# Opening of a decoder-layer kernel: three products side by side, two weights ahead of the second chunk, sums of squares ranked higher, later attention units six steps on

## The chip, the cores and the metric

The kernel runs on one core of one Trainium2 chip. The metric is device time in microseconds (us). Before the change the median of three runs is 1660.32 us (1659.6 to 1661.01). A core has a tensor engine (PE in the profile; PEld is its weight load), a vector engine (DVE), a scalar engine (ACT), GpSimd (POOL) and a sync engine (SP) that here only issues DMAs. Each engine works through its own queue strictly in order; a semaphore holds an instruction until what it reads, or the buffer that it overwrites, is ready.

## What is computed

One step of a hybrid decoder layer, for a prompt of 1024 tokens and, with the same weights, for 8 samples of 8 tokens (1088 columns in all). Cut to what the change touches:

```python
xn = rmsnorm(x, norm1_g)
proj = xn @ w_in
q, k, v, glu_a, glu_b, gate_a, gate_b = jnp.split(proj, SPLIT_IDX, axis=-1)
# branch A: attention over a window of 128, with a sink per head
s = einsum(q, k) * HEAD_DIM ** -0.5;  p = softmax(concat[where(mask, s, NEG_INF), sinks])
branch_a = (p[..., :-1] @ v) @ w_o_attn
# branch B: gated linear unit, causal depthwise convolution of 31 taps
u = glu_a * sigmoid(glu_b)
branch_b = silu(layernorm(dwconv(u))) @ w_pb
h = x + (sigmoid(gate_a) * branch_a + sigmoid(gate_b) * branch_b) @ w_out
...
```

The model is 1024 wide, with 16 heads of 64 (4 key heads); the feed-forward part that follows is 2816 wide.

## The kernel before

**Products.** All arithmetic is fp32. Each fp32 product is made of three matmuls (`mm3`, L200 to L202 in the profile): operands are split in a high part rounded to the tensor engine's fp32r form and the rest, and high x high, low x high and high x low are summed. A weight piece of 128 output channels by 1024 inputs comes by DMA (`wraw`), ACT casts it to `whi` (L181) and DVE subtracts to get `wlo` (L182). A product over one chunk of columns is 8 slices of the inputs x 3 = 24 matmuls into one PSUM bank. There are two rings of four banks: "mm" and "aux".

**Opening (`phase_x`).** The 1088 columns come in chunks of 384, 384 and 320 (c = 0, 1, 2). For each chunk `norm1_raw` makes the split of x times the norm's gain (`xh` on ACT, L263; `xl` on DVE, L264), and `norm1_stats` the squares (ACT, L272) and their running sum over the eight slices (DVE, L274); `rstd_rows` then turns the sum into a row of 1/rms: mean matmuls on PE (L292), a root on ACT and a `RECIPROCAL` on DVE (L310, L311, tile `rows`), matmuls that spread `rows` over all partitions (L296), a copy on ACT (L298, `rstd`). Five first products (glu_b, glu_a, a query piece, gate, a second query piece) are taken of the not yet normalized x, so that PE needn't wait for the norm; their evacuations multiply by `rstd` (L819 `u`, L822 `c`, L827 `qt`, L711 `gt`). Their weights are `whi`/`wlo` twice, then `whix`, `whiy`, and one that is kept in the tile `q`. For c = 0 the first two products run side by side, slice by slice, as the data lands. Later `norm1` scales x itself (DVE, L304), casts (ACT, L305) and subtracts on DVE or POOL (L307), in place, for the products that follow.

**Order.** The program is written as a stream, and a scheduler makes each engine's queue from it by priorities; `with self.later(n)` pushes the instructions inside n places back. The sums and `rstd_rows` stand under `MEAN_LATER[c]` (L277), the convolution's multiply-adds (L480, the "macs", which fill DVE through the whole middle) under `CONV_LATER` = 1200. After this the order is fixed: an engine that waits for one instruction doesn't start the next.

**Attention.** `plan_units` (from L788) lays the attention units of a pass p between the matmuls of the products, in steps of three matmuls. A unit has for each of its two head groups g: `scores` (L356, L357, into two aux banks), the softmax (DVE L327 and L334, ACT L332 and L336), `turn` (four transposes per block of keys on PE, L366, into one aux bank, then ACT writes `pth` and DVE `ptl` from it, L229 and L230), and `mix` (L378, L379). An aux bank is free again when DVE has made `ptl` from it. Unit 0 alone has its turns and mixes put off by `FIRST_WAIT` = (6, 14) steps; the next unit starts `SPACING` = 22 steps (19 in the second pass) behind it.

## Time and profile before

| | value |
|---|---|
| median of three runs | 1660.32 us (1659.6 to 1661.01) |
| the profiled execution's own time | 1659.53 us |
| its span, first to last instruction | 1657.8 us |
| mean granted PE clock | 0.997 |
| PE busy | 1642.9 us, 99% |
| DVE busy | 1336.1 us, 81% |
| ACT busy | 893.3 us, 54% |
| POOL busy | 328.1 us, 20% |

The span is what the trace covers; 1.73 us of the execution lie around it. PE is busy for all but 15 us of it, so the table itself says little: what matters is where these 15 us are, and where the clock was below 1. Those places are found in the list of PE's waits, the timeline of PE and the table of windows, and are shown in the prediction.

### The profile page before, as it was taken

How to read it: one execution, taken by the hardware profiler on the slowest of the kernel's cores; microseconds unless marked ns; L12 is line 12 of the kernel's file. 1: busy time of each engine (PE TensorE's matmuls, PEld its weight loads, DVE VectorE, ACT ScalarE, POOL GpSimd, SP SyncE). 2: the span in 40 equal slices, each digit the busy share in tenths (PEclk: the TensorE clock that was granted, in tenths of full speed). 3: DMA queues.
4: the chain of work that ended last, by engine and by line, in shares of the span. 5: the costliest groups of instructions: out<-in, count | busy, mean ns of one | idle time of the engine just before them, and what ended most of it. 6: DMA issues, size and time to landing. Idle time of an engine off the chain costs nothing.

```text
span 1657.8 us, 30344 instructions
## 1 busy us (share of the span) xinstructions
PE 1642.9 (99%) x11616; PEld 1627.3 (98%) x11616; DVE 1336.1 (81%) x2430; ACT 893.3 (54%) x1817; POOL 328.1 (20%) x589
## 2 busy tenths in 40 slices
PE   9999999999999999999999999999999999999998
PEld 9999999999999999999999999999999999999997
DVE  8899999999769995866685897877777777977556
ACT  7434477753488754993343564444444446834322
POOL 1210114171211211110000123333433220000050
PEclk9999999999999999999999999999999999999999
DMA  6122216254421255545346527676777544857473
GB/s 213 43 52 71 60 63 167 62 178 103 115 67 47 83 195 184 165 137 190 113 136 194 134 79 204 183 182 176 182 176 176 144 112 149 286 157 218 138 148 117
DMA packets 121313, 232.12 MB, mean 140 GB/s; under 512 B 25408, under 2 KB 67536, under 8 KB 120736
## 3 DMA queue, kind: packets, MB, share of 16 engines
q1 hardware_dynamic: 88208, 140.14, 27.6%
q0 software_dynamic: 32384, 89.51, 21.3%
q8 instruction: 91, 1.49, 0.4%
q10 hardware_dynamic: 576, 0.53, 0.1%
q14 instruction: 54, 0.44, 0.1%
HBM read 169.74 MB, written 89.62 MB: 156 GB/s over the span
## 4 chain that ended last, share of the span: by engine, by line
PE 81%; DVE 11%; ACT 4%; issue 2%; DMA 1%; POOL 0%; SPq 0%; DVEq 0%; ACTq 0%; POOLq 0%
PE mm L200 19%; PE mm L202 19%; PE mm L201 19%; PE aux L200 6%; PE aux L202 6%; PE aux L201 6%; DVE c L480 3%; DVE bt L480 2%; PE aux L366 1%; ACT p L332 1%; ACT p L336 1%; PE aux L378 1%; DVE wlo L182 1%; PE aux L356 1%; PE aux L379 1%
## 5 line engine op out<-in xcount | busy, mean ns | idle before, releaser
L200 PE MATMUL mm<-xh,whi 128*128 128x384 f32 (+1 forms) x920 | 306.6, 333 | 0.6 <-ACT whi L181 0.6
L201 PE MATMUL mm<-xl,whi 128*128 128x384 f32 (+1 forms) x920 | 301.1, 327 | 0.0
L202 PE MATMUL mm<-xh,wlo 128*128 128x384 f32 (+1 forms) x920 | 300.7, 327 | 0.0
L200 PEld LDWEIGHTS mm<-xh,whi 128*128 128x128 f32 x920 | 173.3, 188 | 2.2 <-ACT whi L181 1.2
L201 PEld LDWEIGHTS mm<-xl,whi 128*128 128x128 f32 x920 | 173.4, 188 | 1.0
L202 PEld LDWEIGHTS mm<-xh,wlo 128*128 128x128 f32 x920 | 173.1, 188 | 0.1
L1209 DVE SCALAR_TENSOR_TENSOR acc<-st,fc,acc 128x1104 f32<-128x1104 f32 x88 | 119.5, 1361 | 8.7 <-ACT acc L1207 7.9
L181 ACT CAST whi<-wraw 128x1024 fp32r<-128x1024 f32 (+1 forms) x65 | 62.7, 970 | 56.8 <-PE mm L201 44.6
L480 DVE SCALAR_TENSOR_TENSOR bt<-u,consts,bt 128x513 f32<-128x513 f32 x120 | 89.7, 747 | 0.6
L480 DVE SCALAR_TENSOR_TENSOR c<-sm,hsum,c 128x512 f32<-128x512 f32 x120 | 89.4, 745 | 0.5
L182 DVE TENSOR_TENSOR wlo<-wraw,whi 128x1024 fp32r<-128x1024 f32 (+1 forms) x65 | 72.5, 1121 | 20.1 <-ACT whi L181 19.6
L480 DVE SCALAR_TENSOR_TENSOR c<-u,consts,c 128x512 f32<-128x512 f32 x112 | 83.5, 745 | 0.2
L229 ACT CAST wlo<-th 128x512 fp32r<-128x512 f32 x56 | 35.1, 626 | 65.0 <-PE aux L202 41.3
L1378 ACT COPY st<-mm 128x272 f32<-128x272 f32 (+2 forms) x133 | 44.4, 350 | 46.8 <-PE mm L202 46.8
L200 PE MATMUL mm<-th,whi 128*128 128x272 f32 x240 | 69.3, 289 | 0.0
L202 PE MATMUL mm<-th,whi 128*128 128x272 f32 x240 | 69.3, 289 | 0.0
L201 PE MATMUL mm<-tl,whi 128*128 128x272 f32 x240 | 69.1, 288 | 0.0
L332 ACT ACTIVATE p<-p,nm 128x257 f32<-128x257 f32 (+1 forms) x128 | 62.2, 490 | 11.0 <-DVE nm L327 10.1
L1357 DVE TENSOR_TENSOR st<-st,aux 128x272 f32<-128x272 f32 (+2 forms) x95 | 34.2, 378 | 38.5 <-PE aux L202 38.5
L202 PE MATMUL mm<-sh,wlo 128*128 128x384 f32 (+1 forms) x192 | 62.6, 326 | 0.0
L201 PE MATMUL mm<-sl,whi 128*128 128x384 f32 (+1 forms) x192 | 62.6, 326 | 0.0
L200 PE MATMUL mm<-sh,whi 128*128 128x384 f32 (+1 forms) x192 | 62.6, 326 | 0.0
(651 smaller groups left out, 5906.8 us busy)
## 6 DMA issues: line engine op xcount, KB each, us to landing
wraw<-wall SPq DMA_DIRECT2D x87, 512.0 KB, 4.0
d_x<-st POOLq DMA_DIRECT2D x27, 544.0 KB, 4.9
d_wd<-wall POOLq DMA_DIRECT2D x54, 256.0 KB, 6.1
th<-wall SPq DMA_DIRECT2D x18, 512.0 KB, 6.0
wraw<-wall SPq DMA_DIRECT2D x33, 256.0 KB, 4.1
x<-d_x SPq DMA_DIRECT2D x14, 544.0 KB, 4.8
d_x<-acc POOLq DMA_DIRECT2D x9, 816.0 KB, 7.2
d_wo<-wall POOLq DMA_DIRECT2D x24, 256.0 KB, 4.9
```

The source lines that it names most:

```text
L181: self.nc.scalar.copy(h[:, z], r[:, z])
L182: self.nc.vector.tensor_tensor(l[:, z], r[:, z], h[:, z].bitcast(F32), ALU.subtract)
L200: mm(ps, wh, xh, start=first, stop=False, skip_group_check=more)
L201: mm(ps, wh, xl, start=False, stop=False, skip_group_check=more)
L202: mm(ps, wl, xh, start=False, stop=last, skip_group_check=more)
L229: self.nc.scalar.copy(h, src)
L332: nc.scalar.activation(pt[:, j, lo:width + 1], pt[:, j, lo:width + 1], AF.Exp, bias=nm[:, j:j + 1], scale=-1.0, accum_out=den[:, j:j + 1])
L336: nc.scalar.activation(pt[:, j, lo:width], pt[:, j, lo:width], AF.Identity, scale=den[:, j:j + 1])
L480: mac = lambda o, x, w: nc.vector.scalar_tensor_tensor(o, x, w, o, ALU.mult, ALU.add)
L1209: self.last_tap = nc.vector.scalar_tensor_tensor(acc, st[:, k:k + AW], fw(f, k), acc, ALU.mult, ALU.add)
L1357: plus = lambda d, s: nc.vector.tensor_tensor(d, d, s, ALU.add)
L1378: op(d, r(ps))
```

## The change

Four things are altered.

1. In chunk 0 three products run side by side instead of two (`SIDE = 3`). The third weight, which came as one load of 512 KB after all of chunk 0's x, now comes in four pieces beside the first two weights, and is split in four parts instead of two.
2. The loads: after chunk 0, SP issued all four loads of chunk 1, then weights 3 and 4, then chunk 2. Now it issues the first load of chunk 1, the two weights, then the rest of chunk 1 and chunk 2. `norm1_load` becomes a generator for this.
3. `MEAN_LATER` falls from (100, 100, 100) to (90, 95, 60), so the squares' sums and the rows of 1/rms rank higher; `norm1(0)` is called before the products of chunk 2 instead of after those of chunk 1, and `norm1(1)` after the loop.
4. In both attention passes every unit behind unit 0 starts six steps later.

```diff
-MEAN_LATER = (100, 100, 100)
+MEAN_LATER = (90, 95, 60)
 W_PARTS = 4
+SIDE = 3
...
     def norm1_load(self, pp, c):
         o, n = CHUNKS[c]
         xr = self.t(pp, [P, KT, n], f"xr{c}")
         if c == 0:
             self.w_raw += [self.t(self.wp, [P, DM], "wraw", bufs=2) for _ in range(2)]
+            self.w_raw.append(self.t(self.cv, [P, UW], "u", bufs=2)[:, :DM])
+        yield xr
         for k in range(0, KT, 2):
+            if k:
+                yield
...
     def norm1_raw(self, c, xr, xh, xl):
-        parts = list(zip(self.w_parts(W_PARTS), self.w_parts(W_PARTS))) if c == 0 else []
+        parts = list(zip(*[self.w_parts(W_PARTS) for _ in range(SIDE)])) if c == 0 else []
...
                 steps += [(at + d, f) for d, f in new]
-                at += SPACING[p][kind]
+                at += SPACING[p][kind] + (FIRST_WAIT[0] if (kind, n) == ("u", 0) else 0)
...
-        xr = [self.norm1_load(p0, 0)]
+        loads = [self.norm1_load(p0, c) for c in range(3)]
+        xr = [next(x) for x in loads]
+        for _ in loads[0]:
+            pass
         first = COFF["ident"][0]
-        self.raw_slot = lambda i: (self.cv, "u") if i == 2 else (self.wp, "wraw")
-        self.w_load()
+        self.raw_slot = lambda i: (self.wp, "wraw")
         nc.sync.dma_start(self.consts[:, first:], a["consts"][:, first:])
-        xr.append(self.norm1_load(p0, 1))
+        next(loads[1])
         while len(self.w_raw) < FIRST:
             self.w_load()
-        xr.append(self.norm1_load(p0, 2))
+        for x in loads[1:]:
+            for _ in x:
+                pass
...
             rs.append(self.norm1_stats(p0, c, xr[c]))
+            if c == 2:
+                self.norm1(0, xr[0], rs[0], xh, xl)
             self.scale = rs[c]
             evs, tags = (ev_b, ev_a, ev_q(0), gate_evac(*self.order[3]), ev_q(1)), FIRST_TAGS[c]
-            side = 0 if c else 2
+            side = 0 if c else SIDE
...
             if c == 0:
                 self.derive()
-            if c:
-                self.norm1(c - 1, xr[c - 1], rs[c - 1], xh, xl)
+        self.norm1(1, xr[1], rs[1], xh, xl)
         self.norm1(2, xr[2], rs[2], xh, xl)
```

Three places show what this does to the queues. In the names the numbers are the program's buffers; line numbers of the changed kernel are 1 to 10 higher.

The first is ACT's queue as chunk 0 ends and the fourth weight (`whiy`) is needed. `xh_20` is the high part of chunk 0, `xh_22` of chunk 1, `sq` are squares. Before:

```order
L272 ACTIVATE sq_240<-xr_29_126 128x384
L263 ACTIVATE xh_22_106<-xr_33_148,consts_77 128x384
L272 ACTIVATE sq_243<-xr_29_126 128x384
L263 ACTIVATE xh_22_106<-xr_33_148,consts_77 128x384 x7
L310 ACTIVATE rows_248<-aux_247,consts_77 128x3
L181 CAST whiy_211<-wraw_153 128x512 x2
```

Now:

```order
L268 ACTIVATE xh_22_106<-xr_33_130,consts_77 128x384
L277 ACTIVATE sq_244<-xr_29_126 128x384
L277 ACTIVATE sq_247<-xr_29_126 128x384
L182 CAST whiy_218<-wraw_154 128x512 x2
L277 ACTIVATE sq_250<-xr_29_126 128x384
L182 CAST q_26_122<-wraw_156 128x512 x2
L268 ACTIVATE xh_22_106<-xr_33_130,consts_77 128x384 x6
L315 ACTIVATE rows_255<-aux_254,consts_77 128x3
```

The two casts of `whiy` stood behind seven casts of `xh_22` and the root for chunk 0's rows; now they stand ahead of six of those and of the root, and so does the next weight.

The second is DVE's queue ahead of the `RECIPROCAL` of chunk 1's rows. `xr_29` is chunk 0's x, which `norm1` scales in place, `xl_25` the low part of chunk 2, `sq` with 320 columns chunk 2's sum. Before:

```order
L304 SCALAR_TENSOR_TENSOR xr_29_126<-xr_29_126,consts_77,rstd_57_246 128x384 x2
L264 SCALAR_TENSOR_TENSOR xl_25_109<-xr_36_157,consts_77,xh_24_108 128x320
L307 TENSOR_TENSOR xl_21_105<-xr_29_126,xh_20_104 128x384
L264 SCALAR_TENSOR_TENSOR xl_25_109<-xr_36_157,consts_77,xh_24_108 128x320 x4
L274 TENSOR_TENSOR sq_640<-sq_640,sq_638 128x320
...
L274 TENSOR_TENSOR sq_658<-sq_658,sq_655 128x320
L311 RECIPROCAL rows_446<-rows_446 128x3
L819 TENSOR_TENSOR u_162<-aux_456,rstd_76_444 128x384
```

Now:

```order
L309 SCALAR_TENSOR_TENSOR xr_29_126<-xr_29_126,consts_77,rstd_57_253 128x384
L279 TENSOR_TENSOR sq_638<-sq_638,sq_635 128x320
L312 TENSOR_TENSOR xl_21_105<-xr_29_126,xh_20_104 128x384
L279 TENSOR_TENSOR sq_641<-sq_641,sq_638 128x320
L309 SCALAR_TENSOR_TENSOR xr_29_126<-xr_29_126,consts_77,rstd_57_253 128x384 x3
L312 TENSOR_TENSOR xl_21_105<-xr_29_126,xh_20_104 128x384
L309 SCALAR_TENSOR_TENSOR xr_29_126<-xr_29_126,consts_77,rstd_57_253 128x384
L316 RECIPROCAL rows_453<-rows_453 128x3
L312 TENSOR_TENSOR xl_21_105<-xr_29_126,xh_20_104 128x384
L828 TENSOR_TENSOR u_165<-aux_463,rstd_76_451 128x384
```

The reciprocal still stands behind all seven sums of chunk 2 and all eight scalings of chunk 0; what moved is that scalings and sums now alternate, and that one of four low parts of `norm1(0)` left for DVE follows it.

The third is DVE's queue in the first attention unit. `bt` and `c` are the convolution's macs, `ptl_2134` (now `ptl_2141`) is the first turn's low part, whose aux bank a later score matmul on PE takes over. Before:

```order
L334 RECIPROCAL den_2058<-den_2058 128x4
L480 SCALAR_TENSOR_TENSOR bt_1675<-u_1495,consts_77,bt_1675 128x513
L480 SCALAR_TENSOR_TENSOR c_1673<-u_1495,consts_77,c_1673 128x512
...
L480 SCALAR_TENSOR_TENSOR c_1673<-sm_1674,hsum_86,c_1673 128x512
L480 SCALAR_TENSOR_TENSOR c_1673<-u_1495,consts_77,c_1673 128x512
L230 TENSOR_TENSOR ptl_2134<-aux_2128,pth_2133 128x512
L327 ISA p_2140,nm_2152<-aux_2141,masks_945,nsink_84 128x256
```

Now:

```order
L339 RECIPROCAL den_2065<-den_2065 128x4
L485 SCALAR_TENSOR_TENSOR bt_1682<-u_1502,consts_77,bt_1682 128x513
...
L485 SCALAR_TENSOR_TENSOR c_1680<-u_1502,consts_77,c_1680 128x512
L231 TENSOR_TENSOR ptl_2141<-aux_2135,pth_2140 128x512
L485 SCALAR_TENSOR_TENSOR c_1680<-sm_1681,hsum_86,c_1680 128x512
L485 SCALAR_TENSOR_TENSOR bt_1682<-u_1502,consts_77,bt_1682 128x513
L485 SCALAR_TENSOR_TENSOR c_1680<-u_1502,consts_77,c_1680 128x512
L183 TENSOR_TENSOR wlo_210_2163<-wraw_2006,whi_209_2162 128x1024
L231 TENSOR_TENSOR ptl_2176<-aux_2170,pth_2175 128x512
L332 ISA p_2185,nm_2197<-aux_2186,masks_952,nsink_84 128x256
```

Between the reciprocal and the first `ptl` there are eight macs in both. What moved is the score evaluation of the next unit (the `ISA` rows), which now comes after both turns: three macs, a weight's `wlo` and the second `ptl` stand before it.

## The prediction

> **What bounds the kernel now.** I read the page first, then the list of PE's waits, the table of windows around each wait, and the timelines of PE, DVE and ACT there. The page:

> ```profile
> span 1657.8 us, 30344 instructions
> PE 1642.9 (99%) x11616; PEld 1627.3 (98%) x11616; DVE 1336.1 (81%) x2430; ACT 893.3 (54%) x1817; POOL 328.1 (20%) x589
> PE 81%; DVE 11%; ACT 4%; issue 2%; DMA 1%; POOL 0%; SPq 0%; DVEq 0%; ACTq 0%; POOLq 0%
> ```

> The reader is to see that PE stands still for 14.9 us in all, so no regrouping of the same matmuls can win more than that and what the clock lost. The waits (engine, line, what was waited for; total, times, longest):

> ```profile
> PE aux L356 <- DVE ptl L230: 2.3, 2, 2.2
> PE aux L296 <- DVE rows L311: 1.5, 1, 1.5
> PE mm L200 <- ACT whiy L181: 1.2, 1, 1.2
> ```

> The change works on exactly these: 1.2 and 1.5 in the opening, 2.2 at the attention units. A wait can cost more than itself, which the windows show (length; PE, PEld, DVE, ACT, POOL busy; granted clock; DMA share; GB/s):

> ```profile
> 22.00:24.00 2.00, 2.00 (x11) 1.91 (x12) 2.00 (x6) 2.00 (x5) 0.00 (x0) 0.89 1.09 346
> 24.00:26.00 2.00, 2.00 (x8) 2.00 (x7) 2.00 (x4) 2.00 (x5) 0.00 (x0) 0.50 1.08 271
> 26.00:28.00 2.00, 2.00 (x10) 2.00 (x10) 2.00 (x6) 1.51 (x4) 0.00 (x0) 0.76 0.64 180
> 52.00:54.00 2.00, 1.72 (x12) 1.72 (x13) 0.46 (x3) 0.48 (x1) 0.00 (x0) 1.00 0.00 0
> 204.00:206.00 2.00, 1.92 (x10) 1.73 (x9) 2.00 (x8) 2.00 (x9) 0.00 (x0) 0.61 0.00 0
> 206.00:208.00 2.00, 2.00 (x8) 2.00 (x7) 2.00 (x6) 2.00 (x5) 0.54 (x1) 0.53 0.14 59
> ```

> Lost clock is length times (1 minus clock): 0.22 + 1.00 + 0.48 = 1.7 us behind the wait for `whiy`, and 0.78 + 0.94 = 1.7 behind the wait for `ptl`, each half speed for about 3.4 us. The wait for `rows` drew no such stretch: the clock stayed 1.00. So **what can be had** is 1.2 + 1.7, 1.5, 2.2 + 1.7, and at the start some of the two short waits shown below: about 8.5 us, 0.5%.

> [...]

> **The start.** Three products take 9 matmuls per slice of x where two took 6.

> ```profile
> 6.80 0.44 PE L200 MATMUL mm<-xh,whi 128*128 128x384 f32 x1 [0.25 <-ACT whi L181]
> 7.78 0.44 PE L200 MATMUL mm<-xh,whi 128*128 128x384 f32 x1 [0.38 <-ACT whi L181]
> 16.92 0.33 PE L200 MATMUL mm<-xh,whix 128*128 128x384 f32 x1
> 17.10 0.33 PE L201 MATMUL mm<-xl,whix 128*128 128x384 f32 x1
> 16.00:20.00 4.00, 4.00 (x25) 4.00 (x24) 4.00 (x12) 4.00 (x10) 0.16 (x2) 1.00 1.05 400
> ```

> Starts lie 0.173 us apart, so a slice lasts 1.56 us instead of 1.04, and PE asks for x and weights later. The same bytes come (DMA already full, share 1.05), with 512 KB of them moved ahead. I set the start at 0.2 us gained, bounds minus 0.6 (both waits gone) to plus 1 (a late piece of the third weight, about one slice of PE work).

> **The wait for `whiy`.** ACT and PE:

> ```profile
> 17.66 3.64 ACT L263 ACTIVATE xh<-xr,consts 128x384 fp32r<-128x384 f32 x7
> 21.35 1.13 ACT L181 CAST whiy<-wraw 128x512 fp32r<-128x512 f32 x2
> 22.00 0.44 PE L200 MATMUL mm<-xh,whiy 128*128 128x384 f32 x1 [1.24 <-ACT whiy L181]
> ```

> The cast moves ahead of six of the seven `xh` (6 x 0.52 = 3.1 us) and the root, so it ends near 19, with PE arriving at 20.8 as before. Its load now stands ahead of three of chunk 1's four, so it doesn't come late. I cost this wait at nothing: minus 1.24 and minus 1.7. If the load came 2 us late, the 1.2 would be back.

> **Chunk 1's rows.** This is the term that decides the opening. Without the gap, PE reaches these matmuls at about 50.8 (before: 52.28 less 1.46) minus 0.2 minus 2.9, minus five matmuls that now stand behind them (0.9): **46.8**. DVE must by then have run the reciprocal:

> ```profile
> 29.69 0.56 DVE L819 TENSOR_TENSOR u<-mm,rstd 128x384 f32<-128x384 f32 x1 [1.17 <-ACT rstd L298]
> 35.51 1.14 DVE L728 TENSOR_TENSOR q<-qt,q 64x384 fp32r<-64x384 f32 x2
> 37.62 2.96 DVE L304 SCALAR_TENSOR_TENSOR xr<-xr,consts,rstd 128x384 f32<-128x384 f32 x4
> 42.32 0.55 DVE L307 TENSOR_TENSOR xl<-xr,xh 128x384 fp32r<-128x384 f32 x1
> 45.55 2.68 DVE L264 SCALAR_TENSOR_TENSOR xl<-xr,consts,xh 128x320 fp32r<-128x320 f32 x4
> 48.15 3.98 DVE L274 TENSOR_TENSOR sq<-sq,sq 128x320 f32<-128x320 f32 x7
> 52.06 0.17 DVE L311 RECIPROCAL rows<-rows 128x3 f32<-128x3 f32 x1
> 52.28 0.93 PE L296 MATMUL aux<-consts,rows 128*128 128x128 f32 x6 [1.46 <-DVE rows L311]
> 20.00:50.00 30.00, 28.76 (x164) 28.59 (x163) 28.25 (x52) 19.67 (x43) 5.59 (x5) 0.94 0.33 100
> ```

> DVE is busy for 28.25 of these 30 us: it, not the rank of the sums, is what is late. From chunk 0's `u` to the reciprocal 22.4 us pass (29.69 to 52.06). In the new order three more sums of chunk 1 and three more `xl` of chunk 2 stand between these two and one `xl` of `norm1` fewer: by the rows above 3 x 0.57 + 3 x 0.67 - 0.5 = +3.2 us, up to 25.6. The scalings take 0.74 here, with POOL at work beside them; should all eight run at the 0.55 of the `xl` of like size, it is 8 x 0.19 = 1.5 less, 24.1. Chunk 0's `u` itself comes about 4 us sooner: before, it waited for `rstd` until 29.69, and the gap and the lost clock (2.9) and 1.2 of its own wait lay ahead of it; I take 25.6. So the reciprocal falls at 49.7 to 51.2, or at 48 if `u` comes earlier still: I take **49.7**, the end nearest to undisturbed rows. PE waits 2.9 us there instead of 1.5 (bounds 1 and 4.4), and, being longer than the 1.24 that cost clock before, it probably costs the 1.7 as well. PE then passes at 49.9, against 52.28 - 0.9 = 51.4 for the same work: **1.5 us won**, or nothing with the clock.

> **Chunk 2's rows.** The same chain again:

> ```profile
> 72.36 0.17 DVE L311 RECIPROCAL rows<-rows 80x4 f32<-80x4 f32 x1
> 72.97 1.01 PE L296 MATMUL aux<-consts,rows 80*128 80x80 f32 x8
> ```

> They now stand 58 matmuls sooner in PE's queue, at 0.173 x 320/384 = 0.144 each (estimated by columns) 8.4 us: with 0 to 1.5 won, PE comes at 72.97 - 8.4 - 1.5 = 63.1 to 64.6. On DVE, five evacuations, four parts of `q`, eight scalings and three `xl` stand between the two reciprocals, 5 x 0.56 + 4 x 0.57 + 8 x 0.74 + 3 x 0.55 = 12.7 us, so it falls at about 49.7 + 12.7 = 62.4, up to 64.5 if an evacuation waits. The wait is 0 to 1.4. With the start I carry **1 us won** out of the opening, bounds minus 0.5 and 4. The waits removed there come back as waits for DVE.

> **The attention units.** DVE and PE:

> ```profile
> 197.40 0.76 DVE L480 SCALAR_TENSOR_TENSOR bt<-u,consts,bt 128x513 f32<-128x513 f32 x1
> ...
> 202.12 0.75 DVE L480 SCALAR_TENSOR_TENSOR c<-u,consts,c 128x512 f32<-128x512 f32 x1
> 202.79 0.68 DVE L230 TENSOR_TENSOR ptl<-aux,pth 128x512 fp32r<-128x512 f32 x1
> 207.46 1.22 DVE L182 TENSOR_TENSOR wlo<-wraw,whi 128x1024 fp32r<-128x1024 f32 x1
> 203.52 0.38 PE L356 MATMUL aux<-kd,q 128*128 128x256 f32 x1 [2.15 <-DVE ptl L230]
> 50.00:80.00 30.00, 28.54 (x192) 28.23 (x192) 23.01 (x42) 15.97 (x33) 7.97 (x8) 1.00 0.18 58
> 80.00:190.00 110.00, 110.00 (x735) 109.88 (x734) 108.76 (x165) 40.30 (x82) 14.59 (x25) 1.00 0.23 59
> ```

> DVE is full from 80 to 190 (108.76 of 110 us), so whatever stands ahead of `ptl` delays it one for one. Counting the new queue with the durations of these rows, 8.5 us more of work (12 to 13 macs at 0.67) stand ahead of the first `ptl`, since macs are placed sooner; DVE's 7 idle us in 50 to 80 and the 2 before can take nearly all of it. So the first `ptl` starts near 202.5 again. The score that takes its bank moves six steps back, 18 x 0.173 = 3.1 us, and would no longer wait for it. But the later score banks now need the **second** `ptl` too, which stands behind three more macs and a `wlo` (3 x 0.67 + 1.2): 202.5 + 0.6 + 3.2 = 206.3, done at 206.9. PE comes there at about 203.5 (201.4 where it waited before, plus 3.1, less what the opening won, and some transposes and scores change places). It waits **2 to 4 us**, over the length that drew the half clock, against 2.2 before. For the same work: before, PE passed at about 208.8 with its wait and lost clock; now 206.9 and 1.7 of clock, 208.6. So what the opening won is mostly swallowed here, where DVE is the clock: cumulative gain 0 to 1.5, or 3.2 if the clock holds. The second pass moves by six steps likewise, but PE has no wait of 0.3 us there to win.

> **The sum.** 1659.53 (the profiled execution: span 1657.8 and 1.73 around it; 0.8 under the median of 1660.32, within the runs' 1.4) minus 1.0 = **1658.5 us**, no change: below 0.2% (3.3 us), about what a measurement of this kernel can tell.

> **Rivals.**
> *DVE keeps up.* If DVE recovers its idle time sooner (`rows` of chunk 1 by 47, the second `ptl` by 203.5), all three waits and both stretches of lost clock go: 1659.53 - 2.9 - 1.5 - 3.9 - 0.2 = 1651. For it: 1.75 idle us of DVE in 20 to 50 and 7 in 50 to 80; POOL's use stretches DVE's scalings (0.74 against 0.55), which may fall elsewhere. Against it: the counts above. Half of it, say only the attention wait gone, gives 1655.
> *Slower: the second `ptl`.* If a wait of over 3.4 us stands before the second unit's score, with 1.7 us of clock, and one of 4.4 with 1.7 at chunk 1's rows, then PE loses 6.1 + 5.1 where it lost 8.3 (2.9 + 1.5 + 3.9) in all: +2.9, and the later units, which are six steps nearer the end of the pass, give one more such wait (2.2 + 1.7): 1659.5 + 2.9 + 3.9 = 1666. It decides if the second `ptl` starts later than 207.5. Against it: nothing waits after that in the trace except 0.3 us here and there.
> *The loads.* If `whiy` or the third weight comes late, the opening's gap stays: 1659 to 1661, inside the forecast.

> **Chances.** Forecast (within 0.2%): 0.45. DVE keeps up, wholly or by half: 0.37, faster by over 0.2%. Slower by over 0.2%: 0.18. The forecast's own range is 1656.3 to 1662.8; for 8 in 10 it must reach to 1651.5 and to 1664.

> **What would show it.** Right: no wait of PE for `whiy`, clock 1.00 from 22 to 28; a wait at chunk 1's rows of 1 to 4 us, still for DVE's reciprocal, near 46 to 49; a wait for the second `ptl` near 203 to 207 with a clock below 1 behind it. Wrong: a wait for `rows` under 0.5 us, or PE full from 195 to 215 at clock 1.00: then the time is near 1651 to 1655. If `whiy` is waited for again, my reading of the loads was wrong.

## The result: slower by 0.44%, and the profile after

The changed kernel takes 1667.67 us (median of 6 runs, 1666.13 to 1669.55), the kernel before beside it 1660.8 us (6 runs, 1659.6 to 1662.93). The ratio is 1.0044, 95% interval 1.0033 to 1.0055. The interval leaves out 1: it is slower, and its time lies 3.7 us above the upper end of the predicted range. The profiled execution has a span of 1665.5 us, 7.7 more than before.

The page of the changed kernel, the lines that answer to those of before:

```profile
span 1665.5 us, 30349 instructions
PE 1646.9 (99%) x11616; PEld 1628.4 (98%) x11616; DVE 1336.3 (80%) x2432; ACT 892.8 (54%) x1819; POOL 325.0 (20%) x589
```

PE has the same 11616 matmuls, and is busy 4.0 us longer with them and idle 3.7 us longer. The list of PE's waits says where it was idle (engine, line, what it waited for: total, times, longest; some rows left out):

```profile
PE aux L301 <- DVE rows L316: 3.3, 2, 1.9
PE aux L361 <- DVE ptl L231: 2.9, 1, 2.9
PE aux L297 <- DVE sq L279: 1.3, 1, 1.3
...
PE aux L383 <- ACT pth L230: 0.6, 1, 0.6
...
PE mm L201 <- ACT whiy L182: 0.3, 1, 0.3
```

The wait for ACT's `whiy` went from 1.2 to 0.3 us, as the new order of ACT's queue says. In its place PE waits 1.3 us for chunk 0's last sum of squares on DVE, 1.4 and 1.9 us for chunk 1's and chunk 2's `rows`, and 2.9 us for the second `ptl`. All four are waits for DVE. The windows of the changed kernel around them (length; PE, PEld, DVE, ACT, POOL busy; clock; DMA share; GB/s):

```profile
26.00:28.00 2.00, 2.00 (x10) 2.00 (x9) 1.12 (x3) 0.98 (x3) 0.00 (x0) 0.50 1.04 352
52.00:54.00 2.00, 2.00 (x15) 2.00 (x15) 0.56 (x2) 0.49 (x2) 1.01 (x1) 1.00 0.00 0
64.00:66.00 2.00, 0.54 (x4) 0.28 (x2) 2.00 (x3) 1.23 (x4) 1.11 (x2) 1.00 0.00 0
66.00:68.00 2.00, 1.55 (x9) 1.56 (x10) 1.97 (x4) 0.51 (x1) 1.07 (x1) 0.73 0.03 8
68.00:70.00 2.00, 2.00 (x9) 2.00 (x9) 1.46 (x5) 1.90 (x3) 0.84 (x1) 0.50 0.67 205
210.00:212.00 2.00, 0.39 (x4) 0.19 (x2) 2.00 (x4) 0.00 (x0) 0.00 (x0) 1.00 0.20 82
214.00:216.00 2.00, 2.00 (x7) 1.81 (x7) 2.00 (x8) 2.00 (x9) 0.00 (x0) 0.50 0.67 238
```

In the windows where PE stands nearly still (64 to 66, 210 to 212) DVE is busy for the whole 2.00 us. Half clock follows the waits at 22, 64 and 210 us; it doesn't follow the one at 50. Before, there were two such stretches, so the third accounts for 1.7 of the 4.0 us that PE is busy longer. Most of the rest lies in the transposes of `p`, whose group is busy for 36.3 us before and for 38.7 us now:

```profile
L366 PE MATMUL aux<-consts,p 128*128 128x128 f32 x240 | 36.3, 272 | 0.2 <-DVE ptl L230 0.2
L371 PE MATMUL aux<-consts,p 128*128 128x128 f32 x240 | 38.7, 275 | 0.7 <-ACT p L341 0.2
```

At 263 us, for one, four of them take 1.53 us, where four took 0.60 before: they follow ACT, which makes the four parts of `p` that they read one by one in 1.69 us, and which had itself waited 1.91 us for POOL. This part of the loss is not DVE's, and why POOL was late there was not tried.

```profile
262.03 0.52 ACT L337 ACTIVATE p<-p,nm 128x257 f32<-128x257 f32 x1 [1.91 <-POOL p L326]
262.54 1.69 ACT L341 ACTIVATE p<-p,den 128x256 f32<-128x256 f32 x4
263.09 1.53 PE L371 MATMUL aux<-consts,p 128*128 128x128 f32 x4 [0.24 <-ACT p L341]
```

DVE's timeline shows the turn that PE waits for (start, duration):

```profile
208.81 0.69 DVE L231 TENSOR_TENSOR ptl<-aux,pth 128x512 fp32r<-128x512 f32 x1
209.41 0.75 DVE L485 SCALAR_TENSOR_TENSOR c<-sm,hsum,c 128x512 f32<-128x512 f32 x1
...
211.39 1.22 DVE L183 TENSOR_TENSOR wlo<-wraw,whi 128x1024 fp32r<-128x1024 f32 x1
212.53 0.69 DVE L231 TENSOR_TENSOR ptl<-aux,pth 128x512 fp32r<-128x512 f32 x1
```

The first `ptl` starts at 208.81, where before it started at 202.79: 6.0 us later, although the change to the attention units moves nothing ahead of it. PE is late by then too. The first unit, which the six steps don't move, has its first score at 184.57 us before and at 188.96 now, so of the 7.7 us in all 4.4 were lost ahead of the attention:

```profile
184.57 0.28 PE L356 MATMUL aux<-kd,q 128*128 128x256 f32 x1
188.96 0.28 PE L361 MATMUL aux<-kd,q 128*128 128x256 f32 x1
```

### The profile page after: what moved, and what is told of

It is laid out like the page before. It is cut to its first block, busy times and chain, and to the rows that moved or that the text cites. A ratio compares the mean times of both kernels' runs of the same rounds, so it can differ in the third digit from the quotient of the medians.

```text
span 1665.5 us, 30349 instructions
## 1 busy us (share of the span) xinstructions
PE 1646.9 (99%) x11616; PEld 1628.4 (98%) x11616; DVE 1336.3 (80%) x2432; ACT 892.8 (54%) x1819; POOL 325.0 (20%) x589
## 4 chain that ended last, share of the span: by engine, by line
PE 83%; DVE 10%; DMA 2%; ACT 2%; issue 2%; POOL 0%; SPq 0%; DVEq 0%; ACTq 0%; POOLq 0%
PE mm L201 20%; PE mm L203 20%; PE mm L202 19%; PE aux L203 6%; PE aux L201 6%; PE aux L202 6%; DVE c L485 3%; DVE bt L485 1%; PE aux L371 1%; PE aux L383 1%; DVE q L733 1%; PE aux L384 1%; PE aux L361 1%; DVE wlo L183 1%; PE aux L362 1%
## 5 line engine op out<-in xcount | busy, mean ns | idle before, releaser
L201 PE MATMUL mm<-xh,whi 128*128 128x384 f32 (+1 forms) x920 | 306.6, 333 | 0.6 <-ACT whi L182 0.5
L201 PEld LDWEIGHTS mm<-xh,whi 128*128 128x128 f32 x920 | 173.5, 189 | 2.0 <-ACT whi L182 0.8
L182 ACT CAST whi<-wraw 128x1024 fp32r<-128x1024 f32 (+1 forms) x65 | 62.6, 969 | 53.9 <-PE mm L202 48.1
L230 ACT CAST wlo<-th 128x512 fp32r<-128x512 f32 x56 | 35.1, 626 | 65.1 <-PE aux L203 41.4
L201 PE MATMUL mm<-th,whi 128*128 128x272 f32 x240 | 69.3, 289 | 0.0
L201 PE MATMUL mm<-sh,whi 128*128 128x384 f32 (+1 forms) x192 | 62.6, 326 | 0.0
```

What stands on the lines that cost most here:

```text
L182: self.nc.scalar.copy(h[:, z], r[:, z])
L201: mm(ps, wh, xh, start=first, stop=False, skip_group_check=more)
L230: self.nc.scalar.copy(h, src)
```

## The experiments

Each run was timed against the kernel before on the same chip. "Q" in the expectations is the theory that what stands ahead on DVE's queue decides; the rivals are named there. The number of macs ahead of the first `ptl` is counted in each program's DVE queue. A profile is of one execution; those of e5, e6 and e10 took 2.1, 3.4 and 2.1 us less than their medians, so the waits read from them are not all that the median lost.

| run | macs ahead of the first ptl | first ptl, us | time, us | ratio to before, 95% |
|---|---|---|---|---|
| before | 100 | 202.79 | 1659.7 to 1660.8 | 1 |
| changed | 111 | 208.81 | 1667.67 | 1.0044 [1.0033, 1.0055] |
| e1_attn_only | 100 | 201.88 | 1660.45 | 1.0000 [0.9991, 1.0008] |
| e2_open_only | 111 | 208.5 | 1665.20 | 1.0034 [1.0021, 1.0047] |
| e3_side_loads | 100 | 203.64 | 1661.38 | 1.0007 [0.9998, 1.0015] |
| e4_ranks | 111 | 206.8 | 1664.77 | 1.0028 [1.0018, 1.0039] |
| e5_c2_rank_back | 104 | 201.89 | 1661.09 | 1.0007 [0.9998, 1.0016] |
| e6_c2_rank_only | 108 | 206.32 | 1665.52 | 1.0028 [1.0019, 1.0038] |
| e7_rows_later | 102 | 204.19 | 1660.12 | 1.0002 [0.9993, 1.0011] |
| e8_rows_later_12 | 102 | 203.92 | 1661.82 | 1.0015 [1.0006, 1.0024] |
| e9_attn_12 | 100 | 202.97 | 1661.53 | 1.0010 [1.0001, 1.0019] |
| e10_after_hold | 94 | 203.79 | 1661.97 | 1.0013 [1.0004, 1.0021] |
| e11_before_hold | 94 | 201.45 | 1661.46 | 1.0012 [1.0003, 1.0020] |
| e12_c2_back_hold | 94 | 201.31 | 1657.09 | 0.9984 [0.9976, 0.9993] |

### Which part: the change cut in pieces

**e1_attn_only**: the kernel before with only the six steps.

```diff
-                at += SPACING[p][kind]
+                at += SPACING[p][kind] + (FIRST_WAIT[0] if (kind, n) == ("u", 0) else 0)
```

> The kernel before with only the six steps behind the first attention unit. Theory Q (what the ranks put ahead on DVE's queue is what costs at the attention units; the six steps by themselves don't): the first low part of a turn (ptl) runs on DVE near 202.8 us as before, PE no longer waits for it but for the second one, which stands behind three macs and a wlo, near 206.5: a wait of 2 to 3.5 us with about 1.7 us of lost clock, where it was 2.15 and 1.7. Time 1660 to 1662.5, opening unchanged. Rival S (the six steps cause the 4.6 us that the attention units lost): 1664 to 1666.

Measured 1660.45 us, no difference. PE waits 2.3 us for the second `ptl`, which starts at 205.60. Theory Q holds, S falls: the six steps by themselves neither cost nor win; the wait goes from one bank to the next. Two of PE's waits in this run:

```profile
PE aux L356 <- DVE ptl L230: 2.3, 1, 2.3
PE mm L200 <- ACT whiy L181: 1.5, 1, 1.5
```

**e2_open_only**: the changed kernel without the six steps.

```diff
-                at += SPACING[p][kind] + (FIRST_WAIT[0] if (kind, n) == ("u", 0) else 0)
+                at += SPACING[p][kind]
```

> The changed kernel without the six steps: everything of the opening. Theory Q: the first ptl comes as late as in the changed kernel (near 208.8, against 202.8 before), while PE comes to the score that needs its bank near 204.5 already; the wait is 4 to 6 us with 1.7 us of lost clock, and the time is 1666 to 1670, no better than the changed kernel. Rival S (the six steps are what costs): the attention part is as before and the time 1663 to 1664.5, before plus the 3.6 us that the opening lost.

Measured 1665.20 us: between the two forecasts, with the first `ptl` at 208.5 as Q said, but a wait of only 3.0 us, not 4 to 6, because PE itself came late from the opening (at 206). Rival S is too low by 0.7 us and has the first `ptl` wrong. Most of the loss is in the opening's edits. Whether the six steps, which cost nothing alone in e1, cost something on top of these edits is not settled: the changed kernel's median is 2.5 us higher, by the ratios 1.7 us, and the intervals of the two overlap.

**e3_side_loads**: the kernel before with only the three products side by side and the new loads (the edits of the diff in `norm1_load`, `norm1_raw` and `phase_x`). Against the changed kernel that is no six steps, `norm1` called where it was, and

```diff
-MEAN_LATER = (90, 95, 60)
+MEAN_LATER = (100, 100, 100)
```

> The kernel before with the three products side by side and the new order of loads, but with the old ranks, the old place of norm1 and no six steps. Theory Q: ACT and DVE split the fourth and fifth weight ahead of the last two sums of chunk 0 here too, so PE waits 1 to 1.5 us for the last sum (with 1.7 us of lost clock) in place of the 1.24 for whiy; no macs move, so the attention part is as before (first ptl within 1 us of 202.8). Time 1658.5 to 1662. Rival L (the loads and the three products are what made the opening slow, rank or not): 1663 to 1665.

Measured 1661.38 us, at most 0.15% slower. The time and the attention part came as Q said, the place in the opening didn't: there is no wait for chunk 0's last sum, and at most 0.3 us for the fourth weight, but

```profile
PE aux L301 <- DVE rows L316: 3.8, 2, 3.2
PE aux L361 <- DVE ptl L231: 2.4, 2, 2.2
```

chunk 1's rows take 3.2 us where they took 1.5. That is the mechanism by which the prediction gave the opening's gain back, here nearly at its size (2.9). The wait for the last sum belongs to the higher rank together with the loads.

**e4_ranks**: before, with only `MEAN_LATER = (90, 95, 60)` and the new place of `norm1`.

> The kernel before with only the new ranks of the sums (90, 95, 60) and the new place of norm1. Theory Q: eleven more macs stand ahead of the first ptl, DVE runs it 5 to 7 us later than 202.8, PE waits 5 to 8 us there with 1.7 us of lost clock; in the opening the wait for whiy (1.24 and 1.7) stays, and a wait for chunk 2's rows of 1 to 3 us comes. Time 1665 to 1670. Rival L (the loads and the three products cause it): 1659 to 1662.

Measured 1664.77 us, 0.2 under the expected range, with a wait of 3.0 for `ptl` instead of 5 to 8, since PE came late here too (at 204.3). Rival L falls: the ranks, with `norm1` in its new place, make most of the loss, and make it alone.

### Which rank: chunk 2's

**e5_c2_rank_back**: the changed kernel with one number changed.

```diff
-MEAN_LATER = (90, 95, 60)
+MEAN_LATER = (90, 95, 100)
```

> The changed kernel with MEAN_LATER (90, 95, 100): only the rank of chunk 2's sum and rows goes back. Theory Q (a rank that brings a rows matmul forward on PE without bringing DVE's reciprocal forward makes a wait, and it lets macs in ahead of the attention's turns): chunk 2's rows stand 42 matmuls later on PE, so the wait there (2.0 us, and 1.7 of lost clock) goes; 104 instead of 111 macs stand ahead of the first ptl, which falls at 204 to 205.5 instead of 208.8. Time 1660.5 to 1663.5. Rival N (the moved norm1 call and the higher rank of chunks 0 and 1 cost as much): 1665 or more.

Measured 1661.09 us: 6.6 of the 6.9 us are back, by the ratios 6.1 of 7.3. There is one wait for rows (1.9 us, chunk 1), none for chunk 2's, and the first `ptl` is at 201.89, earlier than expected. The count of macs doesn't set its time by itself: with 104 it comes no later here than with 100 in e1. PE's longest waits:

```profile
PE aux L361 <- DVE ptl L231: 2.5, 1, 2.5
PE aux L301 <- DVE rows L316: 1.9, 1, 1.9
PE aux L297 <- DVE sq L279: 1.1, 1, 1.1
```

**e6_c2_rank_only**: the same number the other way round, on the kernel before.

```diff
-MEAN_LATER = (100, 100, 100)
+MEAN_LATER = (100, 100, 60)
```

> The kernel before with MEAN_LATER (100, 100, 60) and nothing else: only chunk 2's sum and rows rank higher. Theory Q: 108 instead of 100 macs stand ahead of the first ptl (5.4 us at 0.67, less what DVE's idle time takes up), which falls at 205 to 207.5; PE waits 3 to 5 us there. At chunk 2's rows PE comes 33 matmuls sooner (near 68) and waits 0 to 2 us. Time 1662 to 1665. Rival N (the moved norm1 call or the ranks of chunks 0 and 1 carry the loss): 1660 to 1661.

Measured 1665.52 us (9 runs, 1661.71 to 1666.43), half a microsecond over the range; the first `ptl` at 206.32 and a longest wait of 3.2 us for it, as Q said, and 2.05 us for chunk 2's rows. Rival N falls. Together e5 and e6 settle it: **chunk 2's 60 instead of 100 is what makes the change slow**, with or without all the rest.

### Why: the wait at the rows and the macs let in

**e7_rows_later**: the loads and three products of e3, with chunk 1's rows pushed back.

```diff
-MEAN_LATER = (100, 100, 100)
+MEAN_LATER = (100, 140, 100)
```

> The run with the three products and the loads alone, with MEAN_LATER (100, 140, 100): chunk 1's rows matmuls stand 25 matmuls (4.3 us) later on PE, while DVE's reciprocal stands where it was. The wait there, 3.2 us with lost clock, should be under 0.5 us, and no other wait of over 1 us come in the opening: PE is 4 to 5 us ahead at 80 us. Theory Q (DVE sets the time at the attention units: it is full from 80 us on, with 102 macs ahead of the first ptl): the first ptl falls at 203.5 to 205.5, PE waits 5 to 7 us there, and the time is 1659 to 1662. Rival F (each wait counts by itself): 1655.5 to 1657.5.

Measured 1660.12 us, as Q said, but not by its way. PE's timeline has the row

```profile
71.54 1.57 PE L301 MATMUL aux<-consts,rows 80*128 80x80 f32 x6 [2.99 <-DVE rows L316]
```

so the 3.2 us at chunk 1 came back as 3.0 us at chunk 2's rows, some 20 us later and before the attention, not there, with 3.4 us of lost clock behind it (clock 0.58, 0.50, 0.50 and 0.71 in the four windows of 2 us from 70 to 78). DVE's reciprocal for chunk 2 ran at 71.33; it is the same queue that is late.

**e8_rows_later_12** is that kernel with twelve steps instead of none behind the first unit, **e9_attn_12** the kernel before with twelve:

```diff
-                at += SPACING[p][kind]
+                at += SPACING[p][kind] + (12 if (kind, n) == ("u", 0) else 0)
```

> The run before this one with every unit behind the first twelve steps later (36 matmuls, 6.2 us). Theory Q: PE has work for these 6 us, but the bank of the second ptl is now the one waited for, near 208.5 to 209.5, where PE comes near 204: a wait of 3 to 5 us; time 1657 to 1660, since it is still DVE that sets the moment. Rival F: no wait left, 1653 to 1656.

> The kernel before with twelve steps instead of the change's six behind the first unit, and nothing else. Theory Q: DVE's queue up to the second ptl is that of the run with six steps, done near 206.3; PE comes there at 206.5 to 207.5: a wait under 0.5 us and no lost clock, where six steps waited 2.3. Time 1655.5 to 1658. Rival P (PE's waits there only move on, as with six steps: no gain): 1659.5 to 1661.

Both missed: 1661.82 and 1661.53 us, no gain and slightly slower. In e9 the second `ptl` was ready at 207.4 and nobody waited for it, but

```profile
PE aux L356 <- DVE av L385: 2.7, 1, 2.7
```

the next score bank is one that `mix` had used, and DVE frees it only with `av`. The DVE timeline of e9 shows what stands before that:

```profile
206.69 0.68 DVE L230 TENSOR_TENSOR ptl<-aux,pth 128x512 fp32r<-128x512 f32 x1
207.29 0.74 DVE L480 SCALAR_TENSOR_TENSOR c<-sm,hsum,c 128x512 f32<-128x512 f32 x1
...
209.94 0.74 DVE L480 SCALAR_TENSOR_TENSOR c<-u,consts,c 128x512 f32<-128x512 f32 x1
210.60 0.67 DVE L385 TENSOR_TENSOR av<-aux,av 64x512 f32<-64x512 f32 x1
```

Five macs, 3.3 us. In both, moving PE's side later only changed which of DVE's results is late; e8 shows the same with a smaller wait (1.0 for `av`, after 3.0 at chunk 2's rows).

**e10_after_hold, e11_before_hold, e12_c2_back_hold** take macs away from ahead of the turns. In the third convolution tile the macs from tap pair 3 on (`range(HOLD, 16)`), and what follows them, are issued only after the first unit's second `ptl`:

```diff
+HELD = 2
+HOLD = 3
...
+        if i == HELD:
+            macs(range(1, HOLD))
+            self.held = lambda: rest(range(HOLD, 16))
+        else:
+            rest(range(1, 16))
...
             live[g][kb] = (ph, pl)
+            if p == 0 and blk == 0 and g == 1:
+                last = [x for x in nc.cur_bb.bb.instructions if x.engine == nc.vector.engine][-1]
+                with self.later(CONV_LATER), self.tc.issue_after(last):
+                    self.held()
```

on the changed kernel, the kernel before, and e5.

> The changed kernel, with the third convolution tile's macs from tap pair 2 on held back until the first attention unit's second ptl: 94 instead of 111 macs stand ahead of the first ptl, nothing else moves ahead of it and the opening is word for word that of the changed kernel. Theory Q (the macs let in ahead are the whole loss at the attention units): the first ptl falls before 204, PE waits under 0.5 us for the banks of both, and the time is 1661 to 1663.5 (the opening's 3.6 us stay lost). Rival B (DVE's total work sets the time, and macs held back are missing later): 1665 to 1668, with new waits between 210 and 300.

Measured 1661.97 us. No wait for `ptl` is left in the list, though the opening is that of the changed kernel:

```profile
PE aux L303 <- DVE rows L318: 3.8, 2, 1.9
PE aux L299 <- DVE sq L281: 1.1, 1, 1.1
```

Q holds, B falls: with these macs out of the way of the turns 5.7 us of the changed kernel's time are gone (5.1 by the ratios). That is more than the 3.3 us that it lost from the first unit's score on, for no wait like the 2.2 us of the kernel before is left there either.

> The kernel before with the same macs held back: 94 instead of 100 ahead of the first ptl. Theory Q: the first ptl falls near 199, PE doesn't wait at 201.4 (2.15 and 1.7 us saved); time 1656 to 1658. Rival B: 1659.5 to 1661.

This one missed: 1661.46 us, a little slower than before. The first `ptl` comes at 201.45, not 199, as ACT is late there, and PE still waits 1.46 us for it; and a wait of 1.25 us that was not there before comes at 480 us:

```profile
198.69 0.75 DVE L486 SCALAR_TENSOR_TENSOR c<-u,consts,c 128x512 f32<-128x512 f32 x1 [2.24 <-ACT c L497]
```

```profile
479.85 0.63 PE L368 MATMUL aux<-consts,p 128*128 128x128 f32 x4 [1.25 <-DVE ptl L232]
```

The first row is DVE's (it waits 2.24 us for ACT to begin a convolution, with `ptl` queued behind), the second PE's. At 480 us it is not the held macs that are late: DVE itself waits there for ACT's `pth`, as it did before. The row of the kernel before, then that of e11:

```profile
478.77 0.69 DVE L230 TENSOR_TENSOR ptl<-aux,pth 128x512 fp32r<-128x512 f32 x1 [1.66 <-ACT pth L229]
479.01 0.69 DVE L232 TENSOR_TENSOR ptl<-aux,pth 128x512 fp32r<-128x512 f32 x1 [1.65 <-ACT pth L231]
```

PE's transposes behind it start at 479.61 before, after a wait of 0.17 us, and at 479.85 in e11, after 1.25: PE came there sooner and gained nothing by it. The time is nearer to B's than to Q's, but not by B's way. On the kernel before, holding these macs alone wins nothing; which of the change's other edits it takes for them to win was not tried.

> The changed kernel with chunk 2's rank back at 100 and the macs held back: the two repairs together. Theory Q: in the opening the waits for chunk 0's last sum (1.1) and for chunk 1's rows (1.9) stay, that for chunk 2's rows is gone; at the attention units no wait of over 0.5 us: 1655 to 1657.5, under both kernels. Rival B: 1659.5 to 1662.

Measured 1657.09 us (11 runs, 1655.12 to 1658.42; ratio 0.9984, 0.9976 to 0.9993): faster than both kernels, by 2.7 us and by 10.6. PE's list of waits has none over 0.2 us left at the units, and the windows of this run at 200 to 204 us have PE at 2.00 of 2.00 at full clock while DVE has time to spare:

```profile
200.00:202.00 2.00, 2.00 (x15) 1.96 (x14) 0.69 (x1) 2.00 (x5) 1.17 (x4) 1.00 0.25 98
202.00:204.00 2.00, 2.00 (x16) 2.00 (x15) 1.74 (x2) 1.14 (x3) 1.01 (x2) 1.00 0.24 98
```

The four kernels with and without the two repairs: 1667.7 (neither), 1661.1 (rank back), 1662.0 (macs held), 1657.1 (both). Each repair is worth 4 to 6.6 us and they nearly add.

## Why the prediction was wrong, step by step

- **What can be had** (8.5 us): right as a bound, and e12, which has no wait at the attention units, won 2.7 of it.
- **The wait for `whiy`**, cost at nothing: right (0.3 us left).
- **Chunk 0's last sum**: the step that was missing. The prediction counted no other wait of PE before chunk 1's rows. In the new queue the splits of the fourth and fifth weight stand ahead of the last two sums on DVE; PE waited 1.3 us for them and lost the clock as well (0.50 in the window of 26 to 28 us shown above), which takes the place of what `whiy` gave back. DVE's rows, then PE's:

```profile
19.67 1.29 DVE L183 TENSOR_TENSOR wloy<-wraw,whiy 128x512 fp32r<-128x512 f32 x2
21.12 1.29 DVE L183 TENSOR_TENSOR q<-wraw,q 128x512 fp32r<-128x512 f32 x2 [0.16 <-ACT q L182]
22.33 0.55 DVE L279 TENSOR_TENSOR sq<-sq,sq 128x384 f32<-128x384 f32 x1
23.33 0.55 DVE L279 TENSOR_TENSOR sq<-sq,sq 128x384 f32<-128x384 f32 x1
23.93 0.61 PE L297 MATMUL aux<-mean,sq 128*128 128x1 f32 x4 [1.34 <-DVE sq L279]
```

- **Chunk 1's rows**: the mechanism was right; predicted reciprocal 49.7, wait 2.9, measured 51.39 and 1.38. PE came 3.4 us later than I had it (50.2), because of the step before, and DVE 1.7 later. DVE's 1.7 are two errors that partly cancel: chunk 0's `u` came at 28.61 instead of 25.6, and from it to the reciprocal passed 22.8 us, not 24.1. No clock was lost here (1.00 from 52 to 54 us), as in the kernel before; the prediction held it for probable.
- **Chunk 2's rows**: mis-sized. "The wait is 0 to 1.4" with no clock; measured 1.91 and, in the windows of 66 to 70 us shown above, 1.5 us of lost clock, the reciprocal at 66.2 instead of 62.4 to 64.5. I counted the scalings ahead of the reciprocal and let the late start of chunk 1's chain, and the wait of `u` for `rstd` (1.44 us on DVE), go uncounted. So the opening, which was to win 1 us, lost 4.4 up to the first unit's score. e5 and e6 show this rank to be the cause.
- **The attention units**: the other large error. "DVE's 7 idle us in 50 to 80 and the 2 before can take nearly all" of the 8.5 us of macs, so that the first `ptl` would start near 202.5. It started at 208.81, 6.0 us later than before: eleven more macs stand ahead of it, and DVE is busy 7.9 us longer up to it, of which idle time took up 1.9. As I now read its timeline, its idle time in the opening is spent waiting for ACT and PE in a fixed order (3.5 us for ACT's `rstd` and 1.2 for PE from 20 to 80 us), and macs placed behind the waiting instruction don't fill it; e10, which takes the macs away and gets the time back, shows the price, not this reason for it. The second `ptl` comes 3.7 us behind the first, as predicted, with half clock behind the wait (0.50 from 214 to 216 us). That the wait of 2.9 lies in the predicted 2 to 4 is luck: the second `ptl` started 6.2 us later than forecast (212.53, not 206.3), and PE came 6.9 us later (210.4, not 203.5). The 208.8 with which the prediction compares is half a microsecond too high as well: 203.52 + 3.1 + 1.7 is 208.3.

DVE's busy time up to the first `ptl` in one window, of the kernel before:

```profile
0.00:202.79 202.79, 196.99 (x1254) 195.43 (x1254) 186.61 (x322) 101.48 (x219) 32.97 (x52) 0.99 0.31 90
```

and of the changed one:

```profile
0.00:208.81 208.81, 202.12 (x1267) 198.78 (x1268) 194.53 (x335) 102.56 (x224) 33.23 (x51) 0.98 0.31 87
```

DVE's idle time up to there fell from 16.2 to 14.3 us only, instead of taking nearly all of the 8.5 us that were counted.

- **The rival nearest to the result** is the slower one, the second `ptl`. Its point of decision, a start later than 207.5, was passed (212.53). That its 1666 us is close to the measured 1667.7 is luck in part: its waits of over 3.4 us here and of 4.4 with lost clock at chunk 1's rows did not come (2.9, and 1.38 without), and what was lost at chunk 0's last sum, at chunk 2's rows and in the transposes of `p` is not in its sum. I gave it and all of the slower side 0.18, because I took the idle time of DVE for room.

## What to carry to other kernels

A rank that brings an instruction forward on the bounding engine is worth nothing unless the engine that feeds it gets there sooner too; look first at what stands ahead in the feeder's queue. When a scheduler fills an engine with low-ranked work, count how many such pieces a change lets in ahead of each result that others wait for, and price them nearly in full: here the filled engine's idle time took up 1.9 of 7.9 us. Removing a wait on the bounding engine by moving its own side can just show the feeder's next late result; here the time fell when the feeder's work was moved and the rank undone.

## What the runs showed of the hardware

Whether an idle stretch of PE costs half clock isn't settled by its length. The wait for `whiy` is the same instruction in several runs: before, 1.24 us of it drew 1.7 us of lost clock; in e4, 1.5 us of it drew none (clock 1.00 in the three windows of 2 us from 22 to 28). At the attention units 2.3 us drew it in e1 (clock 0.61 and 0.54 in the two windows from 206 to 210), and 3.0 us did not in e4 (1.00 in the four windows from 204 to 212).

The traces show how long the stretches are and when they begin. While PE works, they run in the kernel before from 23.55 to 26.96 and from 204.45 to 207.86 us, and in the changed kernel so:

```profile
25.95:29.36 3.41, 3.41 (x14) 3.41 (x14) 1.92 (x5) 2.29 (x7) 0.00 (x0) 0.50 1.00 313
66.91:70.32 3.41, 3.41 (x15) 3.41 (x15) 2.84 (x7) 2.22 (x3) 1.92 (x1) 0.50 0.46 144
213.68:217.10 3.42, 3.42 (x13) 3.23 (x13) 3.42 (x14) 3.27 (x12) 0.54 (x1) 0.50 0.43 149
```

```profile
202.75:206.16 3.41, 1.75 (x12) 1.40 (x10) 3.41 (x7) 0.99 (x3) 2.60 (x2) 1.00 0.28 115
206.16:209.58 3.42, 2.00 (x12) 1.80 (x13) 3.42 (x12) 1.63 (x7) 0.87 (x2) 1.00 0.00 0
```

In e1 2.3 us fall in the window that ends where the half clock begins:

```profile
203.02:206.43 3.41, 1.09 (x9) 0.89 (x7) 3.41 (x6) 0.00 (x0) 0.00 (x0) 1.00 0.01 2
206.43:209.84 3.41, 3.41 (x12) 3.22 (x13) 3.41 (x14) 2.93 (x11) 0.31 (x1) 0.50 0.46 154
```

The 1.24 us of the kernel before also fall in the window ahead of its first stretch, 20.14 to 23.55. The idle time in one window doesn't settle it either: in the same kernel 1.43 us in the window from 50.85 to 54.27 drew none. Whether it counts how a wait is spread over such windows was not shown; what decides it stays open.

For a forecast this means 1.7 us per long wait is a chance, not a price. The times of e6 look like it: five executions of 1665.5 to 1666.4 us have a mean granted clock of 0.995 or 0.996, three of 1661.7 to 1662.8 us one of 0.997 or 0.998. By these figures 0.002 of 1660 us, 3.3 us, or about two such stretches (an estimate), lie between them.
